# Block 0's expert rows in borrowed buffers, 190 of them beside the mixers, with dense tiles over four PSUM banks

## The chip, the cores and the metric

The kernel runs on one core of a Trainium2 chip. Its engines are TensorE (PE in the profile, with its weight loads as PEld), VectorE (DVE), ScalarE (ACT), GpSimd (POOL) and SyncE (SP, which only issues DMAs here). The metric is the device time of one execution in microseconds (us). What counts is the median of several executions.

## The reference

One decoder layer over 512 tokens of width 1024. Three token mixers (FoX attention, sliding-window attention, memory attention) run from one projection, are gated, merged and projected (`x += merged @ w_out`). Behind them stands a product-key expert layer:

```python
def peer_ffn(h, w_q, keys1, keys2, u, v):
    ...
    v1, i1 = lax.top_k(s1, PEER_TOPK)        # 128 keys, 16 best, 8 heads, two halves
    v2, i2 = lax.top_k(s2, PEER_TOPK)
    ...
    sv, si = lax.top_k(cand, PEER_TOPK)      # 16 best of the 256 sums
    experts = e1 * N_KEYS + e2               # 16 experts of 16384 for each head
    gates = jax.nn.softmax(sv, axis=-1)
    ...
        a = jnp.einsum('cd,ced->ce', h_c, u[e_c])
        act = jax.nn.gelu(a, approximate=False) * g_c
        return jnp.einsum('ce,ced->cd', act, v[e_c])
```

Each token so has 8 x 16 = 128 chosen experts, each with a vector `u` and a vector `v` of 1024 numbers.

## The kernel before, in words

**Blocks and stages.** The 512 tokens are four blocks of 128. `mixers(0)` does block 0, then `mixers(1)` does blocks 1 to 3 together. Blocks 0 and 1 take their experts by gathering, blocks 2 and 3 by a dense pass over all 16384 experts.

**Rows.** A *row* is one gather by GpSimd (L876) that fetches one expert vector for each of 128 tokens (128x1024 f32), and one VectorE instruction on what has landed: a dot product with the token (`u`, L891) or a weighted sum (`v`, L898 while the mixers and the early part run, L904 onto a PSUM tile later). A few rows are done *apart*, on ACT and POOL (L886, L887, L894, L895). A block has 128 u rows and 128 v rows, so there are 512 jobs in the list `JOBS`; `step` takes them in order. Row buffers come from the pool `rows`, `ROWS_IN` = 5 of them, and a gather is issued `AHEAD` = 4 jobs before its use.

**Block 0's experts beside the mixers.** `beside()` is a generator which `mixers(1)` pumps at each weight load (`pump`, L79 on). It first runs the search of block 0 (`search`: per head the loads of `keysT`, L744, and of two parts of `w_pq`, L113; 16 matmuls, L752; two score matmuls, L760; copies to SBUF, L756 and L763; the 16 best by VectorE, L717 to L721). Then comes the choice (`weigh`, `numbers_of`: softmax and expert numbers), and then rows, until `EARLY_ROWS` = 176 are done. The search is put out at the priority that it stands at, choice and rows at a lower one (`tc.high_priority(-LATER)`). A scheduler sets the order of the instructions on each engine from these priorities; a few instructions are pinned by `keep_in_program_order`.

**The weights.** A weight tile is loaded raw (SP queue, L113), cast to its high part `whi` (ACT, L119), and the rest `wlo` = raw - whi is formed on VectorE (L131) or on POOL (L129), by the share in `due`. Each product is then three matmuls (L145, L146, L147).

**Behind the mixers.** The buffers of the mixers' pool (`pp`, closed by `pre.close()`) are given back, and the search of blocks 1 to 3 starts in their memory (pool `qb`). The norm of the merged token states ends in the copy `rstd` (L1055); it is followed by the transposed copies of the normed states (L236), the projection and the score matmuls, and VectorE's 16 best. `PER_ROW` = 3.4 us of search work is put out for each row in between. Then weights and expert numbers of blocks 1 to 3 (the *cover*), under which PE runs dense tiles: a dense u tile (`dense_u`, L1040) is 8 fp32 products of 128 experts with the 256 tokens of blocks 2 and 3, into a PSUM bank `mm`, and a gelu on ACT (L1042). `FIRST_U` = 4 such tiles run in the search, `COVER` = 28 in the cover, `DURING` = 25 in the *spread* (L1100 to L1118: the gates of blocks 2 and 3 are spread over the experts). Then the *main* part: 128 dense v steps, the 71 left-over dense u tiles (in split form), and the rows of block 1.

In the profile's stages: mixers(0) to 155 us; block 0's search and choice beside mixers(1) to 242; rows beside mixers(1) to 624; search of blocks 1 to 3 to 748; cover to 827; spread to 980; main to 1547.

Of the kernel before, what the change touches and what calls it, by code (L numbers as in the profile page):

```python
# [7 lines left out]
F32 = mybir.dt.float32  # L8
F32R = mybir.dt.float32r
# [20 lines left out]
FIRST_U, COVER, DURING, AFTER = 4, 28, 25, 0  # L30
PRE_U = 13
KEPT = FIRST_U + COVER
# [21 lines left out]
EARLY_ROWS, PER_ROW, APART, NO_APART = 176, 3.4, 4, 94.0  # L54
# [3 lines left out]
def tile_block(ctx: ExitStack, tc: tile.TileContext, t: dict, out: bass.AP):  # L58
# [21 lines left out]
    def pump(part=1.0):  # L80
        if inside[0]:
            return
        inside[0] = True
        credit[0] += part * PACE[pace[0]]
        while credit[0] > 0:
            if pace[0] == "search":
                cost = next(side[0], None)
            else:
                with tc.high_priority(-LATER):
                    cost = next(side[0], None)  # L90
            if cost is None:
                credit[0] = 0.0
                break
            credit[0] -= cost
        inside[0] = False
# [4 lines left out]
    early, loads = [], [2]  # L100
# [8 lines left out]
    def fill(raw, src, n):  # L109
        if len(src.shape) == 3:  # L110
            nc.sync.dma_start(raw[:, :n].rearrange("p (c w) -> p c w", c=src.shape[0]), src.rearrange("c p w -> p c w"))
        else:
            nc.sync.dma_start(raw[:, :n], src)  # L113
# [133 lines left out]
    for hf in range(2):  # L247
# [3 lines left out]
                                    pp.tile([128, D], F32R, name="ownlo", bufs=1))]  # L251
# [377 lines left out]
    def mixers(g, hT):  # L629
# [10 lines left out]
        fox(g, 1, qT, oT)  # L640
        merged = wide(f"mg{g}", nb)
# [71 lines left out]
    def search(qq, h2T, f, nb, fetch=None):  # L713
# [27 lines left out]
        def scores(h):  # L741
            s = []
            keys = qq.tile([128, 2, NK], F32, tag="keys", name="keys")
            nc.sync.dma_start(keys, t["keysT"][:, 2 * h:2 * h + 2])  # L744
            qp = qq.tile([128, 2, 128 * nb], F32, tag="qp", name="qp")
            if nb == 1:
                ps = bank("mm")[:, :256]
                for half in range(2):
                    pump()
                    w = fetch(t["w_pq"][2 * h + half], D).rearrange("p (k w) -> p k w", k=KC)  # L750
                    for dc in range(KC):
                        PE.matmul(ps[:, half * 128:(half + 1) * 128], w[:, dc], h2T[dc], start=dc == 0, stop=dc == KC - 1)  # L752
                A.copy(qp.rearrange("p i s -> p (i s)"), ps)
            else:
                for half in range(2):
                    A.copy(qp[:, half], gemm_tr(h2T, t["w_pq"][2 * h + half]))  # L756
            for half in range(2):
# [104 lines left out]
    JOBS = [(b, tab, j) for b in (0, 1) for tab in "uv" for j in range(NJ)]  # L862
    known, issued, done, ahead, flying, rpool = [2 * NJ], [0], [0], [AHEAD], {}, []
    begun_v = set()

    def step(apart=False):

        while issued[0] < min(known[0], done[0] + ahead[0] + 1):
# [3 lines left out]
            if ahead[0] > AHEAD and n % (ROWS_IN + MORE) >= ROWS_IN:  # L872
                r = wp.tile([128, WSLOT], F32, tag="raw", name="row")[:, :D]
            else:
                r = rpool[0].tile([128, D], F32, tag="row", name="row", bufs=ROWS_IN)
            G.indirect_dma_start(out=r, out_offset=None, in_=t["peer_" + tab],  # L876
                                 in_offset=bass.IndirectOffsetOnAxis(ap=eidx[b][:, j:j + 1], axis=0))
            flying[n] = r
        n = done[0]
        done[0] += 1  # L880
        b, tab, j = JOBS[n]
        r, c = flying.pop(n), slice(j, j + 1)
        if tab == "u" and b and j == 0:
            A.copy(two[0], h2n[b])
# [27 lines left out]
    def beside():  # L912
# [3 lines left out]
        with tc.tile_pool(name="qa", bufs=2, side="right") as qq:  # L916
# [12 lines left out]

            yield from search(qq, h2T, f, 1, fetch)  # L930
        pace[0] = "choose"
# [8 lines left out]
        rpool.append(ctx.enter_context(tc.tile_pool(name="rows", bufs=1, side="right")))  # L940
        while done[0] < EARLY_ROWS:
            step()
            yield 1.4
# [27 lines left out]
    side[0] = iter(())  # L971
# [45 lines left out]
    def dense_u(k):  # L1017
# [20 lines left out]
        ps = bank("mm")  # L1038
# [331 lines left out]
```

## Time and profile before

| | |
|---|---|
| median of 3 runs | 1570.54 us (1567.91 to 1571.1) |
| profiled execution, its own time | 1565.71 us |
| span in its profile | 1563.9 us (1.8 us lie around it) |
| mean granted TensorE clock | 0.991 |
| busy: PE, DVE, ACT, POOL | 1499.1 (96%), 1420.1 (91%), 812.0 (52%), 779.5 (50%) us |
| read from and written to memory | 516.99 and 14.69 MB, 340 GB/s over the span |

A row of the windows view gives for a stretch of the span the length, each engine's busy time with its instructions in brackets, the granted clock, the busy share of the 16 DMA engines and GB/s. In the timeline a row is start, length, engine, line, operation and tiles; in square brackets at its end stands how long the engine was idle before it, and for what. In the chain of waits a row is start, length and what held the chain. In the view of waits a row is who waited for whom: total, times, longest.

### The profile page before, as it was taken

Reading aid. Unit: us, or ns where it says so; the run is one execution under the profiler, and the core shown is the slowest. Engines: PE = TensorE matmul, PEld = TensorE weight load, DVE = VectorE, ACT = ScalarE, POOL = GpSimd, SP = SyncE. Lnnn points to the kernel's source line nnn. Section 1 sums busy time; section 2 is a strip of 40 time slices with the busy share of each in tenths; the row PEclk is TensorE's granted clock in tenths of the full one; section 3 lists DMA queues with packets and bytes.
Section 4 is the critical chain, followed back from the end, with each engine's and each line's share of the span. In section 5 each row is a group of like instructions: output and inputs, shape, how many; then the busy total and the mean of one; then the engine's idle time right before and its main releaser. Section 6 shows DMA issues by size and latency. Waiting matters only on the chain.

```text
span 1563.9 us, 27116 instructions
## 1 busy us (share of the span) xinstructions
PE 1499.1 (96%) x9411; PEld 1359.7 (87%) x9411; DVE 1420.1 (91%) x2675; ACT 812.0 (52%) x1804; POOL 779.5 (50%) x642
## 2 busy tenths in 40 slices
PE   8999899999998989999999999899999999999998
PEld 7999898997997988899788888788888888888887
DVE  6689387888998999899999998899999999999998
ACT  7778246646445434342117989544454544444443
POOL 1101016767566557786454665555554545545451
PEclk9999999999998999999999999999999999999999
DMA  8688647898998899876998999999999999999995
GB/s 334 227 280 297 241 161 266 321 362 294 333 360 299 301 339 347 312 288 239 327 389 286 388 399 383 365 407 404 403 411 410 404 410 406 406 411 410 410 409 211
DMA packets 180125, 533.48 MB, mean 341 GB/s; under 512 B 17660, under 2 KB 48148, under 8 KB 179988
## 3 DMA queue, kind: packets, MB, share of 16 engines
q0 software_dynamic: 73728, 268.47, 45.5%
q1 hardware_dynamic: 96180, 227.54, 39.9%
q10 hardware_dynamic: 10080, 35.75, 5.7%
q8 instruction: 74, 1.21, 0.3%
q14 instruction: 63, 0.52, 0.1%
HBM read 516.99 MB, written 14.69 MB: 340 GB/s over the span
## 4 chain that ended last, share of the span: by engine, by line
PE 46%; issue 17%; POOL 13%; DVE 12%; DMA 8%; ACT 4%; POOLq 0%; another core or an unknown queue 0%; SPq 0%; DVEq 0%; ACTq 0%
POOL row L876 12%; PE mm L1040 9%; PE mm L146 7%; PE mm L145 7%; PE mm L147 7%; DMA row<-in_peer_v_dram,eidx 3%; DMA row<-in_peer_u_dram,eidx 3%; PE sc L1115 3%; DVE two L904 2%; PE mm L752 2%; DVE wlo L131 1%; PE sc L498 1%; PE tp L376 1%; ACT whi L119 1%; DVE tmp L719 1%
## 5 line engine op out<-in xcount | busy, mean ns | idle before, releaser
L876 POOL DMA_INDIRECT row<-in_peer_v_dram,eidx x256 | 322.1, 1258 | 287.0 <-DVE two L904 162.1
L876 POOL DMA_INDIRECT row<-in_peer_u_dram,eidx x256 | 316.1, 1235 | 237.8 <-DVE scr L891 127.5
L131 DVE TENSOR_TENSOR wlo<-raw,whi 128x1024 fp32r<-128x1024 f32 (+1 forms) x228 | 277.7, 1221 | 20.1 <-ACT whi L119 17.3
L904 DVE SCALAR_TENSOR_TENSOR two<-row,acts,two 128x1024 f32<-128x1024 f32 x196 | 251.6, 1284 | 2.5 <-DMA row<-in_peer_v_dram,eidx 0.2
L119 ACT CAST whi<-raw 128x1024 fp32r<-128x1024 f32 x146 | 152.3, 1049 | 106.8 <-PE mm L146 51.1
L891 DVE SCALAR_TENSOR_TENSOR scr<-row,own 128x1024 bf16<-128x1024 f32 x128 | 156.4, 1222 | 21.2 <-DMA row<-in_peer_u_dram,eidx 20.5
L891 DVE SCALAR_TENSOR_TENSOR scr<-row,two 128x1024 bf16<-128x1024 f32 x117 | 142.2, 1215 | 7.3 <-DMA row<-in_peer_u_dram,eidx 6.3
L1168 ACT CAST ah<-ga 128x256 fp32r<-128x256 f32 x116 | 47.1, 407 | 160.9 <-PE tp L146 131.5
L203 POOL TENSOR_TENSOR rsy<-rsv,mhalf 128x4 f32<-128x4 f32 (+5 forms) x25 | 38.6, 1547 | 175.5 <-DVE rsv L202 174.6
L145 PE MATMUL mm<-hhi,whi 128*128 128x384 f32 x320 | 109.4, 342 | 2.0 <-ACT hhi L237 1.2
L146 PE MATMUL mm<-hlo,whi 128*128 128x384 f32 x320 | 109.5, 342 | 1.5 <-DVE hlo L239 1.5
L147 PE MATMUL mm<-hhi,wlo 128*128 128x384 f32 x320 | 109.4, 342 | 0.0
L1170 ACT CAST whi<-raw 128x1024 fp32r<-128x1024 f32 x96 | 100.2, 1047 | 15.4 <-DMA raw<-in_peer_v_dram 11.3
L146 PE MATMUL sc<-wlo,ah 128*128 128x512 f32 x256 | 100.9, 394 | 5.3 <-DVE wlo L131 4.1
L145 PE MATMUL mm<-whi,hhi 128*128 128x256 f32 (+1 forms) x360 | 102.8, 288 | 2.9 <-DVE g L610 1.9
L146 PE MATMUL mm<-wlo,hhi 128*128 128x256 f32 (+1 forms) x360 | 101.9, 284 | 2.1 <-DVE wlo L131 2.1
L147 PE MATMUL mm<-whi,hlo 128*128 128x256 f32 (+1 forms) x360 | 101.1, 283 | 0.8 <-DVE hlo L668 0.8
L147 PE MATMUL sc<-whi,al 128*128 128x512 f32 x256 | 101.1, 395 | 0.0
L145 PE MATMUL sc<-whi,ah 128*128 128x512 f32 x256 | 100.9, 394 | 0.0
L145 PE MATMUL tp<-whi,ah 128*128 128x512 f32 x256 | 100.7, 393 | 0.0
L146 PE MATMUL tp<-wlo,ah 128*128 128x512 f32 x256 | 100.5, 393 | 0.0
L147 PE MATMUL tp<-whi,al 128*128 128x512 f32 x256 | 100.3, 392 | 0.0
(325 smaller groups left out, 4480.0 us busy)
## 6 DMA issues: line engine op xcount, KB each, us to landing
raw<-in_peer_v_dram SPq DMA_DIRECT2D x96, 512.0 KB
hhi<-in_uT_dram ACTq DMA_DIRECT2D x68, 512.0 KB
raw<-in_w_tr_dram SPq DMA_DIRECT2D x48, 512.0 KB
raw<-in_w_nat_dram SPq DMA_DIRECT2D x40, 512.0 KB
last<-in_peer_v_dram SPq DMA_DIRECT2D x32, 512.0 KB
hhi<-in_uT_dram SPq DMA_DIRECT2D x26, 512.0 KB
raw<-in_w_o_dram SPq DMA_DIRECT2D x24, 512.0 KB
gd<-st SPq DMA_DIRECT2D x24, 512.0 KB
```

Source lines behind the costliest of these rows:

```text
L119: (cast or A.copy)(hi[:, :n * w], raw[:, :n * w])
L131: V.tensor_sub(lo, raw, hi.bitcast(F32))
L145: PE.matmul(ps, lh, rh, start=first, stop=False)
L146: PE.matmul(ps, lh, rl, start=False, stop=False)
L147: PE.matmul(ps, ll, rh, start=False, stop=last)
L876: G.indirect_dma_start(out=r, out_offset=None, in_=t["peer_" + tab], in_offset=bass.IndirectOffsetOnAxis(ap=eidx[b][:, j:j + 1], axis=0))
L891: V.scalar_tensor_tensor(scr, r, 1.0, two[0] if b else h2n[b], op0=OP.mult, op1=OP.mult, accum_out=acts[b][:, c]))
L904: V.scalar_tensor_tensor(two[0], r, acts[b][:, c], two[0], op0=OP.mult, op1=OP.add))
L1040: PE.matmul(ps[:, :TD], w[:, dc], h2f[dc], start=dc == 0, stop=dc == KC - 1)
L1115: PE.matmul(ps[:, u], o[:, 1, u], o[:, 0, u], start=True, stop=True)
L1168: A.copy(ah, a)
L1170: A.copy(hi, raw)
```

## The change

Five edits come together.

- **Row slots.** While `pre_open` holds (until `mixers(1)` is through), a row takes any buffer that is free: the five of `rows`, the tile `ownlo` of the mixers' pool, and, once the second half of FoX is through, two tiles `v` of that pool. So up to eight gathers are in flight instead of five. A row of those past `EARLY_ROWS` may take only a buffer of `rows`. The gathers are held in the order of the jobs.
- **Block 0's search.** Its loads are pinned in program order, and `keys` of a head is loaded behind the head's two `w_pq` parts (`pinned`; the move of L744 holds for the search of blocks 1 to 3 as well, without the pin).
- **Its choice** is put out at normal priority, like the search.
- **190 rows** (`EARLY_ROWS`) instead of 176 beside the mixers, and `PER_ROW` 3.7 instead of 3.4 in the search.
- **Four banks.** In the cover every second pair of dense u tiles goes to the banks `sc` instead of `mm`; `COVER` is 30 instead of 28 and `DURING` 23 instead of 25, so that `LAG` stays 57 and `KEPT` 32.

```diff
-FIRST_U, COVER, DURING, AFTER = 4, 28, 25, 0
+FIRST_U, COVER, DURING, AFTER = 4, 30, 23, 0
-KEPT = FIRST_U + COVER
+KEPT = 32
-EARLY_ROWS, PER_ROW, APART, NO_APART = 176, 3.4, 4, 94.0
+EARLY_ROWS, PER_ROW, APART, NO_APART = 190, 3.7, 4, 94.0
...
-            if pace[0] == "search":
+            if pace[0] != "rows":
                 cost = next(side[0], None)
             else:
                 with tc.high_priority(-LATER):
...
+            ins = nc.sync.dma_start(raw[:, :n], src)
+        if pinned[0]:
+            tc.keep_in_program_order(ins)
...
         fox(g, 1, qT, oT)
+        if g:
+            free.extend(["v"] * 2)
...
             keys = qq.tile([128, 2, NK], F32, tag="keys", name="keys")
-            nc.sync.dma_start(keys, t["keysT"][:, 2 * h:2 * h + 2])
...
                 for half in range(2):
                     A.copy(qp[:, half], gemm_tr(h2T, t["w_pq"][2 * h + half]))
+            ins = nc.sync.dma_start(keys, t["keysT"][:, 2 * h:2 * h + 2])
+            if pinned[0]:
+                tc.keep_in_program_order(ins)
...
+    pre_open = [True]
+    free, held, gathers = deque(), {}, []
+
+    def borrowed(n):
+
+        if n >= EARLY_ROWS and "row" in free:
+            free.remove("row")
+            held[n] = "row"
+        elif n < EARLY_ROWS and free:
+            held[n] = free.popleft()
+        return held.get(n)
+
+    def slot(n):
+
+        tag = held.get(n, "row")
+        if tag == "row":
+            return rpool[0].tile([128, D], F32, tag="row", name="row", bufs=ROWS_IN)
+        return pp.tile([128, D], F32, tag=tag, name="row", **({"bufs": 1} if tag == "ownlo" else {}))
...
-        while issued[0] < min(known[0], done[0] + ahead[0] + 1):
+        while issued[0] < known[0] and (borrowed(issued[0]) if pre_open[0] else issued[0] <= done[0] + ahead[0]):
...
-                r = rpool[0].tile([128, D], F32, tag="row", name="row", bufs=ROWS_IN)
+                r = slot(n)
...
+        if pre_open[0]:
+            free.append(held.pop(n))
...
+            pinned[0] = True
             yield from search(qq, h2T, f, 1, fetch)
+        pinned[0] = False
...
+        free.extend(["row"] * ROWS_IN + ["ownlo"])
         while done[0] < EARLY_ROWS:
...
-    side[0] = iter(())
+    side[0], pre_open[0] = iter(()), False
+    held.clear()
     mixing.close()
...
-        ps = bank("mm")
+        ps = bank("sc" if FIRST_U <= k < FIRST_U + COVER and k % 4 > 1 else "mm")
```

The instruction orders below are those of the two built programs; the lines of the changed one are its own (L113 is L114, L119 is L122, L129 is L132, L744 is L761, L752 is L756, L756 is L760, L763 is L770, L876 is L901, L898 is L929, L1055 is L1090 there).

**SP's queue at the start of block 0's search, before.** `mg_2400` and `raw` are buffers for the parts of `w_pq`; `w_skvf` and `w_nat` are the first weights of `mixers(1)`; what is in brackets is waited for.

```order
L113 DMA mg_2400<-in_w_pq_dram 128x1024 [waits DMAHW2_49]
L744 DMA keys<-in_keysT_dram 128x256 [waits DMAHW3_49,PE_49]
L744 DMA keys<-in_keysT_dram 128x256 [waits DMAHW4_49]
L113 DMA raw<-in_w_pq_dram 128x1024 [waits DMAHW5_49]
L113 DMA raw<-in_w_skvf_dram 128x1056 [waits DMAHW6_49,PE_49]
L113 DMA raw<-in_w_skvf_dram 128x1056 [waits DMAHW7_49,PE_49]
L113 DMA raw<-in_w_nat_dram 128x1024 [waits DMAHW1_49,DMAHW0_49,PE_49]
L113 DMA raw<-in_w_nat_dram 128x1024 [waits DMAHW6_49,DVE_49]
L113 DMA mg_2400<-in_w_pq_dram 128x1024 [waits DMAHW2_49,PE_49]
```

The same place now:

```order
L114 DMA mg_2400<-in_w_pq_dram 128x1024 [waits DMAHW1_49]
L761 DMA keys<-in_keysT_dram 128x256 [waits DMAHW3_49,DMAHW2_49,PE_49]
L114 DMA mg_2400<-in_w_pq_dram 128x1024
L114 DMA raw<-in_w_pq_dram 128x1024 [waits DMAHW4_49]
L761 DMA keys<-in_keysT_dram 128x256 [waits DMAHW5_49]
L114 DMA mg_2400<-in_w_pq_dram 128x1024 [waits DMAHW6_49,DMAHW0_49,PE_49]
L114 DMA mg_2400<-in_w_pq_dram 128x1024 [waits DMAHW7_49,DMAHW1_49,PE_49]
L761 DMA keys<-in_keysT_dram 128x256 [waits DMAHW2_49,PE_49]
```

The first `keys` waits for PE as before; behind it now come parts of `w_pq`, and the four loads of `w_skvf` and `w_nat` have moved behind them (the first `w_skvf` stands 16 places behind that `keys`, before 3).

**VectorE where the search of blocks 1 to 3 starts, before** (L239 is the last split of the norm, L898 a row, L717 the first maximum of the search):

```order
L898 SCALAR_TENSOR_TENSOR mg_2281<-row,acts_213,mg_2281 128x1024
L239 SCALAR_TENSOR_TENSOR hlo<-sc,gcol,hhi 128x384
L1055 COPY rstd<-rsy 128x3
L717 MAX v_7876<-s 128x8 x3
L718 MAX_INDEX ids_7581<-v_7876,s 128x8
L719 MATCH_REPLACE tmp<-v_7876,s 128x128
```

The same place now:

```order
L242 SCALAR_TENSOR_TENSOR hlo<-sc,gcol,hhi 128x384
L929 SCALAR_TENSOR_TENSOR mg_2281<-row,acts_213,mg_2281 128x1024
L1090 COPY rstd<-rsy 128x3
L929 SCALAR_TENSOR_TENSOR mg_2281<-row,acts_213,mg_2281 128x1024 x11
L722 MAX v_7920<-s 128x8 x3
L723 MAX_INDEX ids_7625<-v_7920,s 128x8
```

Eleven rows, the last of the 190, now stand between the copy `rstd` and the first maximum, where there was none. In all 14 more rows are done ahead of that maximum than before; in search and cover together the count is the same (56), and in the main part it is 12 smaller.

**ACT and POOL at the same place.** ACT before (`dg` uses `rstd`; `qp` is the first projected half, copied out of its PSUM bank):

```order
L223 ACTIVATE dg<-cst,rstd 128x128 [waits DVE_49]
L223 ACTIVATE dg<-cst,rstd 128x128
L119 CAST whi<-raw 128x1024 [waits DMAHW3_49,PE_49,Pool_49]
L756 COPY qp<-mm 128x384 [waits DMAHW7_49,DMAHW5_49,PE_49]
L119 CAST whi<-raw 128x1024 [waits DMAHW6_49,PE_49,Pool_49]
L756 COPY qp<-mm 128x384 [waits PE_49]
```

ACT now:

```order
L226 ACTIVATE dg<-cst,rstd 128x128 [waits DVE_49]
L226 ACTIVATE dg<-cst,rstd 128x128
L122 CAST whi<-raw 128x1024 [waits DMAHW3_49,PE_49,Pool_49]
L122 CAST whi<-raw 128x1024 [waits DMAHW4_49,PE_49,Pool_49]
L760 COPY qp<-mm 128x384 [waits DMASW5_49,DMASW7_49,DMASW3_49,DMAHW5_49,DMASW1_49,DMAHW7_49,DMASW0_49,DVE_49]
L760 COPY qp<-mm 128x384 [waits PE_49]
```

The first copy of `qp` now waits for gathers (DMASW) and for VectorE: its tile lies in the memory of row buffers that were borrowed from the mixers' pool, and the VectorE instruction that it waits for is the last of the eleven rows. The first `keys` load of this search waits for the same.

POOL now, from the norm's power on:

```order
L206 TENSOR_TENSOR rsy<-rsv,mhalf 128x3
L901 DMA row<-in_peer_v_dram,eidx_212 128x1024 x2
L132 TENSOR_TENSOR wlo<-raw,whi 128x1024 x2
L901 DMA row<-in_peer_v_dram,eidx_212 128x1024 x7
L132 TENSOR_TENSOR wlo<-raw,whi 128x1024
L733 TENSOR_TENSOR cand<-v_7920 128x3x24
```

Of the seven gathers behind the two `wlo`, the first two are those of the last two early rows; each `wlo` needs its cast `whi`, which on ACT stands behind `dg`.

More of the change, by code (lines that the diff above doesn't have):

```diff
@@ L1 @@
+from collections import deque
 from contextlib import ExitStack
@@ L98, in tile_block @@
     due, share = [0.0], [0.0]
-    early, loads = [], [2]
+    early, loads, pinned = [], [2], [False]
     def load_raw(src, n):
@@ L110, in fill @@
         if len(src.shape) == 3:
-            nc.sync.dma_start(raw[:, :n].rearrange("p (c w) -> p c w", c=src.shape[0]), src.rearrange("c p w -> p c w"))
+            ins = nc.sync.dma_start(raw[:, :n].rearrange("p (c w) -> p c w", c=src.shape[0]), src.rearrange("c p w -> p c w"))
         else:
-            nc.sync.dma_start(raw[:, :n], src)
+            ins = nc.sync.dma_start(raw[:, :n], src)
+        if pinned[0]:
+            tc.keep_in_program_order(ins)
     def load(src, n, w, fetch=None, cast=None):
@@ L250, in tile_block @@
     hT = [chunks(by_k(x)) for x in (ep.tile([128, D], F32R, tag="own", name="own"),
-                                    pp.tile([128, D], F32R, name="ownlo", bufs=1))]
+                                    pp.tile([128, D], F32R, tag="ownlo", name="ownlo", bufs=1))]
     norm_t([xg[:, 0]], xsum, g1, *hT, tags=("tp", "sc", "tp", "sc", "tg", "acc", "mm", "tp"))
@@ L874, in step @@
             else:
-                r = rpool[0].tile([128, D], F32, tag="row", name="row", bufs=ROWS_IN)
-            G.indirect_dma_start(out=r, out_offset=None, in_=t["peer_" + tab],
+                r = slot(n)
+            ins = G.indirect_dma_start(out=r, out_offset=None, in_=t["peer_" + tab],
                                  in_offset=bass.IndirectOffsetOnAxis(ap=eidx[b][:, j:j + 1], axis=0))
             flying[n] = r
+            if pre_open[0] and n:
+                tc.add_manual_dep(ins.ins, gathers[-1], mybir.DependencyInfo(
+                    mybir.DependencyClass.NoSync, mybir.DependencyReason.DATA), reason="rows in order")
+            gathers.append(ins.ins.name)
         n = done[0]
```

## The prediction, made before the changed kernel had run

> **What bounds the kernel now.** I read the page's busy times first, then the windows view by stage, then the waits and the timeline at the places that the change touches.
>
> ```profile
> PE 1499.1 (96%) x9411; PEld 1359.7 (87%) x9411; DVE 1420.1 (91%) x2675; ACT 812.0 (52%) x1804; POOL 779.5 (50%) x642
> 155.00:245.00 90.00, 85.38 (x663) 82.34 (x662) 58.93 (x273) 34.92 (x103) 13.70 (x37) 0.98 0.55 186
> 555.00:640.00 85.00, 74.16 (x515) 70.64 (x514) 77.99 (x93) 33.57 (x65) 57.33 (x39) 1.00 0.94 336
> 640.00:748.00 108.00, 105.44 (x607) 100.96 (x605) 105.01 (x610) 40.35 (x69) 76.43 (x78) 1.00 0.77 278
> 748.00:827.00 79.00, 78.24 (x355) 68.33 (x355) 77.03 (x117) 9.29 (x25) 40.26 (x38) 0.98 0.97 362
> 827.00:980.00 153.00, 145.29 (x898) 131.94 (x897) 139.89 (x204) 135.70 (x502) 88.13 (x71) 0.99 0.99 361
> 980.00:1100.00 120.00, 114.49 (x652) 99.08 (x651) 112.57 (x169) 58.02 (x94) 62.36 (x48) 1.00 1.01 394
> 1100.00:1300.00 200.00, 197.47 (x1155) 173.32 (x1154) 195.03 (x241) 96.25 (x141) 100.49 (x75) 1.00 1.03 408
> 1300.00:1500.00 200.00, 196.13 (x1135) 171.81 (x1134) 198.89 (x202) 95.67 (x139) 103.60 (x76) 1.00 1.03 409
> ```
>
> PE is busy for 96% of the span and the change takes no matmul away, so it can only move PE's idle time. The rows (length, then PE, PEld, DVE, ACT, POOL) say where that is: 4.6 us in block 0's search, 10.8 in the last 85 us of the mixers, 2.6 and 0.8 in search and cover of blocks 1 to 3, 7.7 in the spread, and 5.5 + 2.5 + 3.9 = 11.9 in the main part up to 1500. VectorE is nearly as full from 640 on (105.0 of 108, 77.0 of 79, 198.9 of 200), and the DMA engines are full in the main part. So rows are paid for on VectorE everywhere behind 640, and a delay of the search's first maximum delays all that follows, unless rows done earlier give it back later.
>
> **Block 0's search.** Its start in the waits of SP's queue and in the chain:
>
> ```profile
> SPq L744 <- PE mm L318: 12.2, 1, 12.2
> 163.13 7.17 PE mm L318 x32
> 170.33 4.98 DMA raw<-in_w_skvf_dram
> 175.36 0.95 issue
> 179.12 2.85 PE mm L752 x24
> 181.98 6.53 DMA mg<-in_w_pq_dram
> 188.55 7.25 PE mm L752 x48
> 185.00:195.00 10.00, 7.99 (x57) 7.80 (x57) 5.40 (x40) 0.86 (x3) 1.60 (x8) 0.83 0.88 334
> ```
>
> SP stands 12.2 us at `keys` until PE is through with L318. Then it issues four mixer weights ahead of `w_pq`; ACT's copies for the search stand behind the cast of the first of them, landed at 175.3, and PE waits again for `w_pq` until 188.5. The change leaves the 12.2 us (the first `keys` still waits for PE) and removes the four loads in between. PE's idle time of 4.6 us can go, and with it the lower clock at 185 to 195 (0.83: 1.7 us of 10). That bounds the gain at 6.3. The loss: each later `keys` waits for PE with `w_pq` behind it, and the mixers' first weights now come late; a landing costs at least the 4.98 of the chain, of which the search's own matmuls cover most. I take -5, with -7 and +2 as ends.
>
> The choice at normal priority does nothing that I can find: its VectorE instructions stand in nearly the same order.
>
> **Rows beside the mixers.** Eight slots for five let gathers go earlier. PE's 10.8 us idle at 555 to 640 lie beside rows on a VectorE that is busy for 78 of 85, so fewer waits for landings help little; the number of rows done at each point of the mixers differs by two at most. I take 0, with -9 as the end (a rival).
>
> **The start of the next search.** This is the term that decides. The timeline before:
>
> ```profile
> 628.62 2.38 POOL L129 TENSOR_TENSOR wlo<-raw,whi 128x1024 fp32r<-128x1024 f32 x1
> 628.82 3.28 DVE L898 SCALAR_TENSOR_TENSOR mg<-row,acts,mg 128x1024 f32<-128x1024 f32 x1
> 633.15 1.27 DVE L898 SCALAR_TENSOR_TENSOR mg<-row,acts,mg 128x1024 f32<-128x1024 f32 x1
> 636.17 0.17 DVE L1055 COPY rstd<-rsy 128x3 f32<-128x3 f32 x1 [1.22 <-POOL rsy L203]
> 637.91 0.47 ACT L756 COPY qp<-mm 128x384 f32<-128x384 f32 x1
> 638.08 4.74 POOL L129 TENSOR_TENSOR wlo<-raw,whi 128x1024 fp32r<-128x1024 f32 x2 [0.75 <-ACT whi L119]
> 638.43 0.94 PE L760 MATMUL sc<-keys,qp 128*128 128x128 f32 x6 [0.44 <-ACT qp L756]
> 639.55 0.34 PE L147 MATMUL mm<-hhi,wlo 128*128 128x384 f32 x1
> 639.73 0.34 PE L145 MATMUL mm<-hhi,whi 128*128 128x384 f32 x1
> 640.84 0.68 DVE L717 MAX8 v<-s 128x8 f32<-128x128 f32 x3 [4.50 <-ACT s L763]
> ```
>
> and the gathers in the chain of the stretch before it:
>
> ```profile
> 610.31 0.95 POOL row L876
> 611.26 0.74 issue
> 612.23 7.34 DMA row<-in_peer_v_dram,eidx
> ```
>
> `qp` is copied at 637.9, PE goes on with scores and the next projection at 638.4, and VectorE's first maximum is at 640.8. Now the first `qp` copy waits for the last of 190 rows. Step by step: three more rows stand ahead of `rstd`, 3 x 1.27 = 3.8 us, less part of the 1.22 us idle there: `rstd` at 639. POOL's two `wlo` follow it as now, 1.9 us later and 4.74 us long: 641 to 645.7. Behind them come the gathers of the last two rows, the second issued one gather (0.95) later, at 646.8. From issue to landing the chain shows 612.23 + 7.34 - 610.31 = 9.3 us: 656.1. The row itself: 657.4. Then `qp` (0.47), at 658. (VectorE is not what is late: eleven rows from 639 on are 14.0 us, to 653.) PE's order has 35 matmuls of the third projection ahead of the first scores, and the first of them waits for the bank that this copy frees: 35 x 0.18 (639.73 - 639.55) = 6.3 us, the scores 0.94, the copy to SBUF and the start of the maximum (640.84 - 639.37 before) 1.5: 667. So the search begins 26 us late. The low end is +16: rows without a wait end at 653.0, and from `qp` to the maximum the old 2.9 us. The high end is +30, with two rows as long as the 3.28 at 628.82.
>
> The Trainium skill, "SBUF: State Buffer", section "Who interferes with whom", says that a VectorE instruction with two SBUF inputs and a GpSimd instruction that reads SBUF exclude each other for the whole instruction. The trace agrees (3.28 beside a `wlo` of 2.38, against 1.27 alone). By it the eleven rows would last 14.0 + 4.7 = 18.7 us and end at 657.7 instead of 657.4, so the sum would be 0.3 us later.
>
> The same skill, "TensorE: Matmul & The Clock Gate", section "What's actually happening", says that an idle window of about 3.4 us halves PE's clock until one busy window has passed. The trace has 0.83 for ten us after PE's wait at 182 to 188, which agrees in size. PE would idle some 17 us here; by the rule the 35 matmuls begin at half clock, and the sum would be 1.7 us later.
>
> **Search and cover.** The rows in them are the same 56, and VectorE is full, so they keep their length. The new banks and tiles in PE's timeline:
>
> ```profile
> 748.76 11.45 PE L1040 MATMUL mm<-h2f,ga 128*128 128x256 f32 x44 [3.32 <-ACT ga L1042]
> 823.07 3.62 PE L1040 MATMUL mm<-h2f,hhi 128*128 128x256 f32 x16
> 830.33 1.32 PE L1115 MATMUL sc<-o 128*128 128x128 f32 x8 [3.31 <-issue]
> ```
>
> A tile is 16 passes, 3.6 us. The banks can take away the 3.32 us for which PE waits for a gelu at 745, two more tiles cost 7.2, and PE has 3.31 idle at the end, where VectorE's choice is late. 7.2 - 3.3 - 3.3 = +0.6, under VectorE's delay: 0 (ends -3 and +3). The spread so starts at -5 + 26 = +21.
>
> **What comes back.** The spread has two tiles fewer: 7.2 us of PE, against 7.7 us of PE idle and VectorE at 139.9 of 153. I take -5 (ends -2 and -7). The main part has 12 rows fewer:
>
> ```profile
> L904 DVE SCALAR_TENSOR_TENSOR two<-row,acts,two 128x1024 f32<-128x1024 f32 x196 | 251.6, 1284 | 2.5 <-DMA row<-in_peer_v_dram,eidx 0.2
> PE mm L147 <- DVE ulo L1029: 5.0, 6, 1.6
> PE mm L147 <- DVE u L1029: 4.7, 7, 1.1
> ```
>
> 12 x 1.284 = 15.4 us of VectorE and 12 x 0.524 MB (128 x 1024 x 4 bytes) at 408 GB/s = 15.4 us of transfers. But PE must do all its matmuls there and idles for 11.9 us only, of which it waits 9.7 for VectorE's splits. So -12 is the end, 0 the other, and I take -7.
>
> Sum: -5 + 26 - 5 - 7 = +9. On the profiled execution, 1565.7, that is 1574.7. It lies 4.8 us under the median of the runs; the forecast is for the median: 1570.5 + 9 = 1579.5, in round numbers 1579.
>
> **The rivals.**
>
> *Returned in full (faster).* The place is the main part: if the rows set its pace (DMA share 1.03, VectorE 198.9 of 200), all of PE's idle time there goes, -12, and -7 in the spread; and the start of the search costs only its low end, because the gathers land in time. +16 - 5 - 7 - 12 = -8: 1562.5. It decides from the point at which the start costs less than the 24 us that the other terms give. For it: the splits that PE waits for are VectorE's. Against it: the two gathers behind two `wlo`. 0.26.
>
> *Nothing returned (slower still).* PE's work is the floor of spread and main: +26 - 5 - 2 - 2 = +17: 1587.5. For it: 197.5 of 200. 0.14.
>
> *The slots help the mixers.* 9 of the 10.8 us at 555 to 640 go, and cancel the +9: 1570.5. Against it: nearly the same order there. 0.10.
>
> *The change doesn't do what it says* holds for one edit, the priority, and is in the forecast at 0. The rest of the chance goes to two rivals together: both gains (1553.5, 0.06) and block 0's search at +2 with the start at +30 (1590.5, 0.02).
>
> **How the numbers follow.** The forecast has 0.42; its own range is 1574 to 1586. Runs of this kernel tell a difference of about 0.2%, 3.1 us. Slower: 0.42 + 0.14 + 0.02 = 0.58, less 0.02 for a forecast that ends within 3.1: 0.56. Same: the slots' 0.10 and those 0.02, less 0.01 on the faster side: 0.11. Faster: 0.26 + 0.06 + 0.01 = 0.33. The range reaches to the full return with its lower neighbours and to nothing returned with the start at +30: 1558 to 1592.
>
> **What would show it.** In the profile after: PE idle for 15 us or more ahead of the third projection, behind ACT's first `qp` copy; the first L722 at about 660, that is 26 - 5 later than 640.8; eleven rows ahead of it, the last two landing some 10 us after two `wlo`; no `w_skvf` ahead of `w_pq` in the chain near 175; no wait of PE for a gelu at 745; the spread beginning 21 us later and the main part 12 us shorter in sum with it. It would be wrong if the first `qp` copy is not waiting for a row, or if PE's idle time in the main part goes entirely.

## The result, and the profile after

| | before | changed |
|---|---|---|
| median | 1570.42 us (1565.45 to 1571.81, 6 runs) | 1586.22 us (1581.89 to 1589.71, 6 runs) |
| profiled execution, span | 1565.7, 1563.9 us | 1589.7, 1587.9 us |

The ratio is 1.010, with a 95% interval of 1.0084 to 1.0115: slower by 15.8 us, where 8.5 were forecast. The changed kernel's profiled execution lies 3.5 us above its median, that of before 4.7 below its own, so of the 24.0 us between the two spans 8.2 are the two executions' own. Below, one of the six executions of experiment 5 took 3059 us and is left out of its ratio.

The windows of the changed kernel at about the places of the earlier ones (length, then PE, PEld, DVE, ACT, POOL; granted clock, DMA share, GB/s):

```profile
162.00:252.00 90.00, 84.12 (x665) 81.15 (x664) 57.94 (x271) 34.88 (x103) 14.67 (x38) 1.00 0.54 188
558.00:643.00 85.00, 76.10 (x505) 72.59 (x504) 81.96 (x94) 31.06 (x60) 53.94 (x39) 0.94 0.93 335
643.00:671.00 28.00, 10.16 (x54) 9.97 (x53) 17.08 (x12) 5.07 (x9) 18.44 (x11) 0.63 0.64 217
671.00:856.00 185.00, 182.54 (x957) 168.20 (x955) 183.14 (x728) 48.01 (x90) 112.20 (x112) 1.00 0.87 318
856.00:1010.00 154.00, 146.46 (x891) 132.87 (x892) 139.16 (x215) 136.81 (x509) 89.59 (x73) 0.96 0.97 354
1010.00:1110.00 100.00, 92.79 (x499) 78.99 (x499) 87.62 (x131) 44.44 (x68) 46.27 (x35) 0.97 0.99 374
1310.00:1510.00 200.00, 199.71 (x1165) 175.57 (x1165) 198.22 (x202) 97.87 (x143) 100.49 (x73) 1.00 1.03 408
```

The third row is new: 28 us in which PE works for 10 and VectorE for 17. The last row shows where something comes back: PE is idle for 0.3 us of 200, where it was 3.9 (from 1327 on, which is as far behind the start of the main part as 1300 was, it is 0.3 as well). But the row above it loses 7.2 of 100 at the start of the main part. The timeline of the third row's stretch, VectorE, ACT, POOL and PE:

```profile
641.78 0.17 DVE L1090 COPY rstd<-rsy 128x3 f32<-128x3 f32 x1 [0.77 <-POOL rsy L206]
641.86 17.14 DVE L929 SCALAR_TENSOR_TENSOR mg<-row,acts,mg 128x1024 f32<-128x1024 f32 x10
659.58 1.29 DVE L929 SCALAR_TENSOR_TENSOR mg<-row,acts,mg 128x1024 f32<-128x1024 f32 x1 [0.58 <-DMA row<-in_peer_v_dram,eidx]
645.35 5.97 POOL L132 TENSOR_TENSOR wlo<-raw,whi 128x1024 fp32r<-128x1024 f32 x2
653.54 1.00 POOL L901 DMA_INDIRECT row<-in_peer_v_dram,eidx  x1 [0.30 <-issue]
660.90 0.86 ACT L760 COPY qp<-mm 128x384 f32<-128x384 f32 x2 [16.34 <-DVE mg L929]
661.43 0.69 PE L148 MATMUL mm<-hhi,whi 128*128 128x384 f32 x1 [17.84 <-ACT qp L760]
670.88 0.68 DVE L722 MAX8 v<-s 128x8 f32<-128x128 f32 x3 [10.02 <-ACT s L770]
```

The ten rows, the two `wlo`, the late gathers, ACT's 16.34 us before the first `qp`, and PE's 17.84 behind it stand there in the order that was forecast; the first maximum is 29.1 us behind `rstd`, against 4.7 before. The `wlo` and the last gather come later than forecast, though, and the ten rows last longer: the eleventh row waits only 0.58 us for its landing.

For what follows, this table cuts each profile by the same instructions of the timeline: the first matmul of block 0's search; the mixers' last merge; `rstd`; the first maximum of the second search; the spread's first instruction on VectorE (L1100); its last matmul (L1115); the end. It gives the us of each stage; the numbers in front are those of the experiments below. (The time to the first matmul varies from execution to execution: 174.1 in before, the earliest, and 176.3 to 183.5 in the others.)

| kernel | mixers beside block 0 | to rstd | to first maximum | search and cover | spread | main |
|---|---|---|---|---|---|---|
| before | 449.2 | 12.8 | 4.7 | 187.7 | 154.5 | 580.8 |
| changed | 445.3 | 15.4 | 29.1 | 184.9 | 154.6 | 577.5 |
| 10: changed, again | 443.4 | 15.4 | 29.4 | 184.9 | 155.1 | 579.6 |
| 1: 176 rows, all the rest | 441.8 | 9.4 | 6.3 | 188.4 | 150.8 | 582.5 |
| 2: tail in own buffers | 445.4 | 14.4 | 7.3 | 204.9 | 152.1 | 572.4 |
| 3: banks alone | 448.0 | 12.8 | 4.7 | 188.5 | 151.4 | 580.6 |
| 4: search alone | 452.9 | 12.8 | 4.7 | 188.4 | 152.5 | 582.2 |
| 5: 190 rows alone | 451.1 | 13.6 | 2.6 | 214.9 | 153.3 | 569.6 |
| 6: 12 rows fewer | 447.5 | 12.8 | 4.7 | 187.9 | 153.7 | 567.2 |
| 7: slots alone | 444.4 | 8.1 | 6.6 | 187.9 | 152.7 | 580.6 |
| 8: slots and banks | 447.1 | 8.1 | 6.6 | 188.4 | 150.6 | 580.3 |
| 9: 12 more rows in the search | 453.7 | 12.8 | 4.7 | 213.1 | 150.8 | 569.3 |
| 11: slots and banks, 182 | 446.8 | 14.6 | 9.8 | 186.2 | 158.6 | 571.8 |
| 12: slots and banks, 170 | 443.2 | 6.8 | 7.9 | 188.5 | 163.4 | 588.1 |

From before to changed that is +7.0 ahead of the first matmul, -3.9, +2.6, +24.4, -2.8, +0.1 and -3.3: +24.1, which is the difference of the spans (24.0) but for rounding.

### The profile page after: what moved, and what is told of

The parts are those of the page before. It is cut to its first block, busy times and chain, and to the rows that moved or that the text cites. A ratio compares the mean times of both kernels' runs of the same rounds, so it can differ in the third digit from the quotient of the medians.

```text
span 1587.9 us, 27087 instructions
## 1 busy us (share of the span) xinstructions
PE 1510.7 (95%) x9411; PEld 1372.0 (86%) x9411; DVE 1427.7 (90%) x2673; ACT 812.0 (51%) x1806; POOL 786.1 (50%) x641
## 4 chain that ended last, share of the span: by engine, by line
PE 78%; DVE 7%; DMA 5%; issue 5%; ACT 3%; POOL 1%; SPq 0%; DVEq 0%; POOLq 0%; ACTq 0%
PE mm L149 12%; PE mm L148 11%; PE mm L150 11%; PE mm L1075 8%; PE sc L149 3%; PE sc L150 3%; PE tp L148 3%; PE tp L149 3%; PE sc L148 3%; PE sc L1075 3%; PE tp L150 3%; PE sc L1150 3%; DVE wlo L134 2%; PE mm L756 1%; PE tp L379 1%
## 5 line engine op out<-in xcount | busy, mean ns | idle before, releaser
L901 POOL DMA_INDIRECT row<-in_peer_v_dram,eidx x256 | 330.1, 1289 | 292.5 <-DVE two L935 164.5
L901 POOL DMA_INDIRECT row<-in_peer_u_dram,eidx x256 | 315.0, 1230 | 234.6 <-DVE scr L922 126.8
L134 DVE TENSOR_TENSOR wlo<-raw,whi 128x1024 fp32r<-128x1024 f32 (+1 forms) x228 | 277.7, 1221 | 25.6 <-ACT whi L122 17.1
L935 DVE SCALAR_TENSOR_TENSOR two<-row,acts,two 128x1024 f32<-128x1024 f32 x186 | 238.8, 1284 | 3.0 <-DVE two L935 0.8
L122 ACT CAST whi<-raw 128x1024 fp32r<-128x1024 f32 x146 | 152.3, 1050 | 114.6 <-PE mm L149 59.9
L922 DVE SCALAR_TENSOR_TENSOR scr<-row,two 128x1024 bf16<-128x1024 f32 x114 | 138.4, 1214 | 2.0 <-DMA row<-in_peer_u_dram,eidx 1.1
L148 PE MATMUL mm<-hhi,whi 128*128 128x384 f32 x320 | 111.2, 347 | 19.4 <-ACT qp L760 17.8
```

The lines of the kernel that those rows point to most:

```text
L122: (cast or A.copy)(hi[:, :n * w], raw[:, :n * w])
L134: V.tensor_sub(lo, raw, hi.bitcast(F32))
L148: PE.matmul(ps, lh, rh, start=first, stop=False)
L901: ins = G.indirect_dma_start(out=r, out_offset=None, in_=t["peer_" + tab], in_offset=bass.IndirectOffsetOnAxis(ap=eidx[b][:, j:j + 1], axi ...
L922: V.scalar_tensor_tensor(scr, r, 1.0, two[0] if b else h2n[b], op0=OP.mult, op1=OP.mult, accum_out=acts[b][:, c]))
L935: V.scalar_tensor_tensor(two[0], r, acts[b][:, c], two[0], op0=OP.mult, op1=OP.add))
```

## The experiments

Each ratio is to runs of the kernel before on the same chip; kernel 1 is that of experiment 1, and so on.

**1. 176 rows, all the rest of the change.**

```diff
-EARLY_ROWS, PER_ROW, APART, NO_APART = 190, 3.7, 4, 94.0
+EARLY_ROWS, PER_ROW, APART, NO_APART = 176, 3.4, 4, 94.0
```

> The changed kernel with 176 early rows and 3.4 us of search per row as before; borrowed slots, pinned search, four banks stay. Theory W (the wait: the search of blocks 1 to 3 starts in memory that borrowed row buffers still hold, so the first qp copy waits for the last early row) and theory R (the rows themselves: 14 rows more on VectorE ahead of the search's first maximum are the cost, whoever waits) both expect the loss gone: 1568 to 1573 us, and the first maximum within 5 us of the mixers' last merge plus 18. A third theory, B (the banks or the pinned search carry the loss), expects 1580 or more.

Measured: 1561.34 us, ratio 0.9950 (0.9934 to 0.9966). The loss is gone, and more than either theory expected: without the 14 rows the change is a gain of 8.6 us. So the rows, or what hangs on them, cost 24.9 us by the medians (1586.22 - 1561.34, on two chips) and 23.6 by the two ratios.

**2. The last 14 early rows in the pool's own five buffers.**

```diff
+TAIL = 14
...
-        if n >= EARLY_ROWS and "row" in free:
+        if n >= EARLY_ROWS - TAIL and "row" in free:
...
-        elif n < EARLY_ROWS and free:
+        elif n < EARLY_ROWS - TAIL and free:
```

> The changed kernel, but the last 14 of the 190 rows may take only the five buffers of the pool rows, so that the mixers' pool is free before them. The first qp copy then no longer waits for the last early row; four rows stay ahead of the first maximum and the rest follow among the search. Theory W expects most of the loss gone: 1568 to 1575 us, PE idle for under 5 us ahead of the third projection. Theory R expects no or little change from the changed kernel: 1581 to 1587 us.

Measured: 1571.65 us, ratio 1.0016 (0.9999 to 1.0033), inside theory W's range: 14.6 us less than the changed kernel. PE waits for no more than 0.6 us at the place of the 17.84. But the table says that it isn't as simple. The stretch from last merge to first maximum is 22.8 us shorter (21.7 for 44.5), and search and cover are 20.0 longer (204.9 for 184.9). The rows now stand among the search, and hold it up there. What is left of the gain lies in the spread (2.5) and above all in the main part (5.1).

**3. The banks alone.**

```diff
-FIRST_U, COVER, DURING, AFTER = 4, 28, 25, 0
+FIRST_U, COVER, DURING, AFTER = 4, 30, 23, 0
-KEPT = FIRST_U + COVER
+KEPT = 32
-        ps = bank("mm")
+        ps = bank("sc" if FIRST_U <= k < FIRST_U + COVER and k % 4 > 1 else "mm")
```

> The kernel before with the four banks and 30 and 23 dense tiles alone. By the prediction's terms: the wait of 3.3 us for a gelu at 745 gone, two tiles (7.2 us) under a cover that ends with VectorE, and 5 us less spread: 1563 to 1567 us. Rival: the spread does not get shorter by less PE work, since its length comes from ACT's and VectorE's steps (as the changed kernel's trace suggests, where it kept its length): 1568 to 1572 us.

Measured: 1566.74 us, ratio 0.9989 (0.9975 to 1.0003), inside the first range, though the interval reaches no change. The spread is 3.1 us shorter in the profile, not 5; and the kernels with the old banks have 150.8 to 154.5 us there, so that one profile hardly tells it.

**4. Block 0's search loads alone.**

```diff
+            ins = nc.sync.dma_start(raw[:, :n], src)
+        if pinned[0]:
+            tc.keep_in_program_order(ins)
...
-            nc.sync.dma_start(keys, t["keysT"][:, 2 * h:2 * h + 2])
...
+            ins = nc.sync.dma_start(keys, t["keysT"][:, 2 * h:2 * h + 2])
+            if pinned[0]:
+                tc.keep_in_program_order(ins)
...
+            pinned[0] = True
             yield from search(qq, h2T, f, 1, fetch)
+        pinned[0] = False
```

> The kernel before with the pinned loads of block 0's search, and keys behind the projection, alone. The prediction's term: 5 us less, 1563 to 1567 us. Rival, from the changed kernel's trace: each later keys waits on SP for PE's scores with w_pq behind it (12.5 us in 6 waits), so PE waits for w_pq twice and nothing is gained: 1568 to 1573 us.

Measured: 1571.30 us, ratio 1.0008 (0.9989 to 1.0027): nothing gained. The changed kernel shows why, in the waits of SP's queue and in the chain:

```profile
SPq L761 <- PE mm L321: 12.8, 1, 12.8
SPq L761 <- PE sc L767: 12.5, 6, 3.5
189.52 5.01 DMA mg<-in_w_pq_dram
206.47 8.61 DMA mg<-in_w_pq_dram
```

The first wait stays (12.8 for 12.2). The transfer of `w_skvf` is gone from the chain, but each later `keys` waits for PE's scores with `w_pq` behind it, and the chain goes through two transfers of `w_pq` (5.01 and 8.61), where it had one (6.53). Kernel 4's own trace has the same: 12.5 us of SP's waits at the first `keys`, 11.6 in six at the later ones, and two transfers in the chain (4.63 and 8.74). PE itself waits 3.0 us there for `w_pq`, in three times, against 2.0 in one before, and 1.6 us once for `keys`.

**5. 190 rows alone, five slots.**

```diff
-EARLY_ROWS, PER_ROW, APART, NO_APART = 176, 3.4, 4, 94.0
+EARLY_ROWS, PER_ROW, APART, NO_APART = 190, 3.7, 4, 94.0
```

> The kernel before with 190 early rows and 3.7 us of search per row alone, in its five buffers: no borrowed memory, so the first qp copy waits for no row. Theory W (the wait for borrowed memory is the cost) expects 1565 to 1573 us. Theory R (the rows themselves: 14 more rows are done ahead of the spread, each 1.7 to 2.3 us long in the form that sums into SBUF beside GpSimd, and the main part gives back less) expects some 10 us more than before: 1577 to 1585 us.

Measured: 1585.67 us, ratio 1.0095 (1.0072 to 1.0118). No row buffer is borrowed here, no `qp` waits for a row, and the loss is as large. Theory W falls as the only cause. The 12 rows that run among the search make search and cover 27.2 us longer, 2.3 us each; the main part gives 11.2 back. Two readings of this kernel: its VectorE rows between 640 and 860 us, by shape, and PE's waits in the same stage.

```profile
L904 DVE SCALAR_TENSOR_TENSOR two<-row,acts,two 128x1024 f32<-128x1024 f32 x56 | 71.9, 1284 | 3.9 <-DMA row<-in_peer_v_dram,eidx 3.5
L898 DVE SCALAR_TENSOR_TENSOR mg<-row,acts,mg 128x1024 f32<-128x1024 f32 x15 | 29.4, 1957 | 0.0
```

```profile
PE mm L1040 <- ACT ga L1042: 10.9, 2, 10.1
PE mm L147 <- POOL wlo L129: 5.3, 2, 4.3
```

A row that still sums into SBUF takes 1957 ns here in the mean, one that sums into PSUM 1284, and PE waits for a `wlo` of POOL, which it did not in the kernel before at this stage.

**6. The price of rows in the main part.** The kernel before without 12 of block 1's 128 weighted sums (they are left out of its output):

```diff
 JOBS = [(b, tab, j) for b in (0, 1) for tab in "uv" for j in range(NJ)
+        if not (b == 1 and tab == "v" and 100 <= j < 112)]
```

> The kernel before with 12 of block 1's 128 weighted sums left out (so its output lacks them): the price of 12 rows in the main part by itself. The prediction's term expects 7 us less, 1563 us; the changed kernel's own main part, shorter by 3.4 us in its profile, 1566 to 1567 us; if the rows set the pace of the main part, up to 15 us less, 1555 us.

Measured: 1554.90 us, ratio 0.9903 (0.9882 to 0.9924), 15.2 us less: 1.26 per row. Rows do set the pace there. The main part of before, of this kernel, of 190 rows alone, and of the changed kernel's second profile:

```profile
983.10:1563.90 580.80, 562.13 (x3230) 490.18 (x3228) 561.21 (x665) 270.41 (x399) 282.31 (x209) 1.00 0.99 393
```
```profile
983.80:1551.00 567.20, 558.99 (x3230) 489.24 (x3228) 546.39 (x653) 271.72 (x399) 269.74 (x197) 1.00 0.99 392
```
```profile
1014.20:1583.80 569.60, 560.17 (x3230) 489.63 (x3228) 545.63 (x639) 272.21 (x399) 270.94 (x196) 1.00 0.99 388
```
```profile
1004.50:1584.10 579.60, 563.95 (x3223) 491.71 (x3221) 545.62 (x639) 271.57 (x399) 268.58 (x197) 0.99 0.98 382
```

PE has some 560 us of work in all of them. With 12 rows fewer VectorE has 546 instead of 561, and PE's idle time falls from 18.7 to 8.2 and 9.4. The changed kernel has the same 546, and PE idles for 15.6. The rows that the change takes out of the main part are of the other kind, dot products (13 by the traces: 85 on VectorE before, 72 now): kernel 5 gets 11.2 us for them.

**7. The slots alone.** The kernel before with `borrowed`, `slot` and their lists as in the change, 176 rows.

> The kernel before with the borrowed row slots alone, 176 early rows. The prediction's term (0, the slots do nothing for the mixers) expects 1568 to 1572 us. Rival: the mixers behind the first row get shorter by 4 to 7 us, as the profiles of the three kernels with the slots show between the first product of block 0's search and the last merge: 1562 to 1566 us.

Measured: 1565.83 us, ratio 0.9973 (0.9958 to 0.9987), the rival's range. The mixers are 4.8 us shorter and the stretch to `rstd` 4.7, where three rows were left and now is none. One profile's mixers can lie 3 us off, but the groups don't meet: 441.8 to 447.1 us in the kernels with the slots, 447.5 to 453.7 in those without.

**8. Slots and banks.** Kernel 7 with the edit of kernel 3.

> The changed kernel with 176 early rows and 3.4 us, without the pinned search, the moved keys and the changed priority of the choice: slots and four banks. If the search's edits gain nothing, 1559 to 1563 us, like the kernel with 176 rows and all the rest (1561.3); if they are part of its gain, 1564 to 1568 us.

Measured: 1559.26 us, ratio 0.9927 (0.9906 to 0.9948), 10.8 us under before, the fastest of the kernels that do all the work. The search's edits and the choice's priority are no part of the gain.

**9. The same rows ahead of the spread, in the other form.** `PER_ROW` 2.35 instead of 3.4 in the kernel before: 12 more rows run in the search and sum into PSUM.

> The kernel before with 176 early rows, but 2.35 instead of 3.4 us of search per row: 12 more rows are done ahead of the spread, as with 190 early rows, but in the form that sums into PSUM. Theory S (the dear thing is the form: a row that sums into SBUF takes 1.7 to 2.3 us beside GpSimd's work on the weights and holds that work up, against 1.28 us for one that sums into PSUM) expects 12 x 1.28 = 15 us lost ahead of the spread and 15 given back: 1567 to 1575 us. Theory R (any row ahead of the spread costs more than it gives back) expects 1578 us or more, like the 1585.7 of 190 early rows alone.

Measured: 1580.02 us, ratio 1.0048 (1.0028 to 1.0068), 8.7 us more. Theory S's number fails: search and cover are 25.4 us longer, 2.1 per row, nearly as with the SBUF form. The rows are short now, but VectorE waits for them:

```profile
L904 DVE SCALAR_TENSOR_TENSOR two<-row,acts,two 128x1024 f32<-128x1024 f32 x196 | 252.4, 1288 | 12.6 <-DMA row<-in_peer_v_dram,eidx 10.3
```

Before, these waits were 2.5 us in all, so 12 rows of 1.288 and 10.1 us more of waits are 25.6. In kernel 5 it is 12 rows of 1.957, 23.5 of its 27.2 us. So 12 more rows in this stage cost 2.1 to 2.3 us each, mostly by a stretched instruction in the one form and by late landings in the other; 1.28 was the price that the prediction knew.

**10. The changed kernel again.**

> The changed kernel itself once more, for a second profile and more runs beside the kernel before. If the 5 us that its first profile shows lost in the first 60 us of the main part belong to the kernel, they stand here again and the main part is again some 577 us long; if they were that execution's, it is 569 to 573 us, as with 190 rows in the other two kernels. The time: 1583 to 1589 us either way.

Measured: 1585.92 us, ratio 1.0086 (1.0059 to 1.0113). The main part is 579.6 us: what it loses at its start belongs to the kernel. The chain there:

```profile
1013.00 11.27 DMA raw<-in_peer_v_dram
1024.35 1.07 ACT whi L1205
...
1030.57 9.90 DMA raw<-in_peer_v_dram
1040.55 1.05 ACT whi L1205
1041.59 0.95 ACT u L1062
1042.57 1.24 DVE u L1064
1043.85 0.58 PE mm L150
```

The first parts of the dense v table land late, and PE waits for what is made from them. In before and in kernel 2 no such transfer is in the chain at this place. In kernel 1, which has 176 rows, there is one (982.64, 10.91 us), so such a transfer doesn't take the 14 rows. The clock is part of the loss: in the first three stretches of 20 us of the main part it was 0.91, 0.95 and 0.88 here and 1.00 in kernel 2, and PE is busy for 563.95 us of the main part against kernel 2's 559.56.

**11 and 12. Slots and banks with 182 and with 170 rows.**

> The kernel with slots and four banks alone (1559.3 us with 176 early rows), with 182 early rows. Theory S: five of the six more rows are done beside the mixers, where VectorE still has room, one or none ahead of the first maximum, and the main part gives back 6 x 1.28 = 7.7 us: 1552 to 1558 us. Theory R: each early row beyond 176 costs about 1 us in sum: 1563 to 1567 us.

> Slots and four banks alone, with 170 early rows: the other side of 176. No row is left between the mixers' last merge and the copy rstd. If each row that is moved out of the early part saves what the step from 176 to 182 cost (8.7 us for six, 1.4 each), 1551 us. If the price is paid only by rows behind the mixers' last merge, the stretch from the last merge to the first maximum gets some 5 us shorter and the main part gets 6 x 1.28 = 7.7 us longer: 1559 to 1563 us.

Measured: 1567.94 us, ratio 0.9980 (0.9963 to 0.9996), and 1578.44 us, ratio 1.0062 (1.0041 to 1.0083). The first is just above theory R's range; the second is far outside both expectations. Kernel 12's twelve runs fall into two groups, six from 1572 to 1577 us and six from 1580 to 1585, and its profile (1580.88) is of the upper one. In both kernels the main part moves as experiment 6 says (-8.5 and +7.8 us for six rows), the stretch from last merge to first maximum goes by +9.7 and 0.0, and the spread gets 8.0 and 12.8 us longer, which nobody expected. There the chain of waits holds a store, once in kernel 12 and once in kernel 11:

```profile
912.73 18.52 DMA gd<-st
```
```profile
886.59 16.71 DMA gd<-st
```

`st` is the buffer of spread gates that ACT fills from PSUM; while its store is under way, ACT can't refill it, and PE can't go on. PE's waits for it in the spread, kernel 12 and kernel 8:

```profile
PE sc L1147 <- ACT st L1153: 13.9, 6, 6.6
```
```profile
PE sc L1147 <- ACT st L1153: 6.0, 5, 2.4
```

The store in the chain doesn't tell the two from the others, however. Kernel 8 has one of 16.69 us there, kernels 1 and 3 have two each (15.5 to 18.0), and their spreads are among the shortest. What differs besides PE's waits is its clock. The spread's rows of before, of the changed kernel, of kernel 8 and of kernel 11:

```profile
828.60:983.10 154.50, 148.38 (x919) 134.79 (x920) 139.79 (x207) 137.63 (x508) 90.39 (x73) 0.99 0.98 357
```
```profile
855.80:1010.40 154.60, 146.86 (x894) 133.27 (x895) 139.37 (x216) 136.81 (x509) 90.19 (x73) 0.96 0.96 353
```
```profile
830.70:981.30 150.60, 142.77 (x894) 130.06 (x895) 139.39 (x205) 136.25 (x507) 89.78 (x74) 0.99 0.99 362
```
```profile
836.00:994.60 158.60, 147.52 (x894) 133.60 (x895) 139.97 (x210) 135.98 (x506) 89.36 (x72) 0.96 0.95 344
```

For the same 894 matmuls PE is busy for 147.52 us in kernel 11, at a clock of 0.96, and for 142.77 in kernel 8, at 0.99: 4.8 of the 8.0 us. Kernel 12 has 147.68 at 0.95: 4.9 of the 12.8. The rest is idle time. No run here separates what comes first, the waits or the lower clock.

So 176 is better than six more or six fewer. With 182 the price lies in the stretch to the first maximum and in the spread, with 170 in the spread and the main part.

## Why the prediction was right

The direction and the term that decides were right, and so was its mechanism in the main: the first `qp` copy waits for the last of the rows. Inside that term two steps erred in opposite ways, and four of the other terms were wrong, of which one, the slots, took back part of what the others added. That the time lies between 1558 and 1592 us says little, as these ends are a gain of 12 and a loss of 22 us; the forecast's own range, 1574 to 1586, was just missed. From the first matmul of block 0's search on, the first profile is 17.1 us longer, not 9: the spread gave 5.1 less than forecast, the main part 3.7 less, block 0's search, the mixers and the start of the next search together cost 2.1 more, and search and cover 2.8 less.

- **Block 0's search, -5: wrong.** Experiment 4 gives no gain. The step that failed is that PE's 4.6 us of idle time can go and that the search's own matmuls cover most of a late landing: each later `keys` holds up SP, and PE idles for 5.9 us in the first of the windows above.
- **Rows beside the mixers, 0: wrong.** The rival of the slots had the better of it: -4.2 us by experiment 7, in the mixers and in the stretch to `rstd`.
- **The start of the search, +26: right.** From last merge to first maximum the two profiles of the changed kernel have 44.5 and 44.8 us, before 17.5: +27.0 and +27.3. PE's wait fits (17.84 for "some 17"), and ACT's copy stands behind the last of the eleven rows. The steps before it fit in sum only, and that is luck. The last gather was issued 11.8 us behind `rstd`, not 7.8, because the two `wlo` began later and lasted 5.97 us, not 4.74; but it was through 6.0 us after its issue, not 9.3. "VectorE is not what is late" failed: two of the ten rows took 3.25 us beside the `wlo`, the other eight 1.28 to 1.34, so that VectorE was busy until 659.0 and the landing held it for 0.58 us alone. (Two such rows were the reason for the high end of +30; by the prediction's own steps they would have ended ahead of the landing and added nothing.) The term is also the sum of two prices, the rows and the wait for borrowed memory. Without the wait most of its time comes back as a longer search (20.0 of 22.8 us in experiment 2). By the medians the rows in their own buffers cost 12.4 us (kernel 2 against 8), or 15.6 (kernel 5 against before), and the borrowed memory 14.6 more (changed against kernel 2).
- **Search and cover, 0:** -2.8, inside the ends.
- **The spread, -5: too large.** 154.6 and 155.1 us, against 154.5, with two tiles fewer on PE. Where the banks stand without the 190 rows it is -3.1 and -3.9 (kernels 3 and 8 against before). The two tiles are gone from PE's work (919 to 894 matmuls), but at a clock of 0.96 instead of 0.99 the rest takes longer: 146.86 us of the 148.38 stay, where kernel 8 has 142.77. In the changed kernel's second profile (PE 145.90, clock 0.97) the chain goes through a store of `st` as well:

```profile
934.33 14.34 DMA gd<-st
```

- **The main part, -7: -3.3 and -1.2.** Twelve weighted sums are worth 13.6 to 15.2 us by experiment 6, and the moved dot products 11.2 by kernel 5, so the end of -12 was about what can be had or somewhat too small; PE idles there for 18.7 us and not for 11.9 (the prediction left out the last 64 us of the windows). The changed kernel doesn't collect it: its main part starts late on its weights and at a lower clock (experiment 10).

What stays open: why the main part of the changed kernel starts late on the v table and that of kernel 2 doesn't, which differs from it only in the buffers of the last 14 rows. Both had moved the same 258 MB by the start of the spread (301 GB/s over 855.8 us, 303 over 850.9). Open is also why the spread gets longer with 182, 190 and 170 rows than with 176 in kernels 1 and 8. The rival "returned in full" is right in size for the main part alone (11.2 to 13.6 us in kernels 5, 9 and 6), but not for the kernel, as kernels 5 and 9 show: both get it back and are slower than before.

In sum: 14 rows ahead of the spread (12 in kernel 9) cost 22 to 26 us there in four kernels (last merge to spread: the changed one and 2 against 1, 5 and 9 against before), and gave back 5 to 11.5 in the main part. The slots and banks give 11 us, which the 14 rows more than use up.

## What to carry to other kernels

Work that is moved between two stages has two prices, and both must be measured: a row cost 2.1 to 2.3 us where it went and saved 0.9 to 1.4 where it came from, though its instruction takes some 1.2 or 1.3 us when nothing holds it up. A buffer that is borrowed from a pool ties the next user of that memory to the borrower's last instruction; end the loan some work earlier, and price what then runs in its place. When a bundle of edits loses, take it apart: two of five edits gave 0.7%, and a third lost more than that.

## What the runs showed of the hardware

The row that sums into SBUF has two SBUF inputs, and its mean length depends on what GpSimd does beside it. The group over the whole kernel, before and changed:

```profile
L898 DVE SCALAR_TENSOR_TENSOR mg<-row,acts,mg 128x1024 f32<-128x1024 f32 x48 | 66.2, 1379 | 1.9 <-DMA row<-in_peer_v_dram,eidx 1.4
```
```profile
L929 DVE SCALAR_TENSOR_TENSOR mg<-row,acts,mg 128x1024 f32<-128x1024 f32 x62 | 89.9, 1450 | 1.4 <-DMA row<-in_peer_v_dram,eidx 0.6
```

The 14 further ones took 23.7 us, 1.69 each. Row by row it is clearer: of the 62 in the changed kernel, the 55 that meet no `wlo` of POOL take 1.27 to 1.34 us; of the seven that overlap with one, two take 1.28, and five take 2.7 to 4.1. The two `wlo` of POOL beside the ten rows took 5.97 us instead of 4.74, so there both sides got longer. In kernels 2 and 5 only the rows did (1.59 and 1.52 us in the mean, 1.38 before): a `wlo` of POOL takes 2.42 us there in the mean, as before. The form that sums into PSUM stays at 1284 to 1288 ns in every kernel.

That two SBUF inputs and GpSimd's reads are in each other's way is what the Trainium skill says in "SBUF — State Buffer", section "Who interferes with whom". The trace agrees: the prediction's sentence on it had 18.7 us for the run of rows, and from 641.86 to 660.87 they took 19.0, of which 0.58 was a wait.

In the chains of the changed kernel's second profile and of kernels 11 and 12, a store inside the spread took 14 to 18.5 us from issue to landing, while the DMA engines moved some 365 to 400 GB/s. Over all of kernel 12 the median of these stores is 11.7 us, and that of a gather 7.8 or 8.2.

After PE's 17.8 us of idle time its matmuls first start 0.32 us apart and from 665.66 on 0.18, and the granted clock was 0.63 over the 28 us around it:

```profile
664.80 0.52 PE L149 MATMUL mm<-hlo,whi 128*128 128x384 f32 x1
665.12 0.52 PE L150 MATMUL mm<-hhi,wlo 128*128 128x384 f32 x1
666.01 0.34 PE L148 MATMUL mm<-hhi,whi 128*128 128x384 f32 x1
666.19 0.34 PE L149 MATMUL mm<-hlo,whi 128*128 128x384 f32 x1
669.51 1.50 PE L767 MATMUL sc<-keys,qp 128*128 128x128 f32 x12
```

The matmuls ahead of the scores so took 8.1 us (661.43 to 669.51), where the prediction's own step had 6.3. The prediction's sentence on the Trainium skill, "TensorE: Matmul & The Clock Gate", section "What's actually happening", put 1.7 us on top, and the trace agrees with its 1.8. From the scores to the first maximum it took 1.4 us and not 2.4, so that the whole came out at 9.4, where the sum had 8.7.
